# One head load of the last group's own columns, split final sums and shorter bookkeeping in a prefix-sum diagonal kernel

## The chip, the cores and the metric

The kernel runs on one core of one Trainium2 chip. The metric is the device time of one execution in microseconds (us). Of several executions the median is quoted. A profile is one more look at a single execution, whose own time is given beside it. Its engines are TensorE (PE in the lines, PEld for its weight loads), VectorE (DVE), ScalarE (ACT), GpSimd (POOL) and SyncE (SP).

## The reference, cut to what matters

```python
def setup_inputs():
    B, H, W = 4, 4224, 4224
    return {"x": np.random.randn(B, H, W).astype(np.float32)}

def reference(x):
    ps = np.cumsum(np.cumsum(x, axis=1), axis=2)
    diag = np.diagonal(ps, axis1=1, axis2=2)
    return np.cumsum(diag, axis=1).astype(np.float32)
```

Output i of a batch is a sum over the diagonal of the 2-D prefix sum. The kernel never forms the prefix sums. It needs the sum of what each diagonal step adds, which are a column's upper part and a row's left part, and adds those up twice.

## The kernel before

Rows come in strips of 768 (6 blocks of 128), cast to bf16 by the load. Per strip VectorE masks the diagonal block, TensorE sums columns with a one-column selector, and ScalarE and VectorE share the row sums. Eleven groups of 384 columns lie in the rows of one PSUM tile `d`, from which a batch's outputs are made.

The last batch is handled so that little is left after its last byte. Its last 384 rows come last, in small pieces: two blocks of 128 rows (`part_a`), and the last 128 rows as four quarters with each row cut in four (`part_b`). Some of their values come early instead, in a `head` at the very start and in `diag_b`.

```python
    HC = 528
    src_a = x[LB, T0:TB, :].rearrange("(h p) w -> p h w", p=P)
    head = last.tile([P, 2, HC], FP32, name="head")
    nc.sync.dma_start(out=head, in_=src_a[:, :, N - HC : N])
    ...                                   # three strips are prefetched
            if not whole and s == 0:
                diag_b = last.tile([P, P], BF16, name="diag_b")
                nc.gpsimd.dma_start(out=diag_b, in_=x[b, TB:N, TB:N])
```

In the lines, `arows` is the sum of each row of the two blocks, `by` comes from quarter 0 of the last rows, `bsum` from 1 and 2, `esum` from 3, and a *pair sum* (`pair`) is VectorE's sum of a piece, whose halves it adds in one instruction. `dump` is scratch. Row sums of the two blocks are shared. TensorE folds some columns onto 256 by identity matmuls (`fold_a`), ScalarE sums others, VectorE the rest:

```python
            cp, ca = c0 + 768, c0 + 768 + 1152
            fold_in(fold_a, part_a, c0, cp, 256, start=True)      # TensorE
            for h in range(2):
                act_sum(asum[:, h, 1:2], part_a[:, h, cp:ca])     # ScalarE
            row_sums(asum[:, :, 2], part_a[:, :, ca:c1])          # VectorE
```

At the end all row sums are weighed (multiplied by how many times each enters an output) by matmuls into one PSUM tile `fin` and added to the rest. The 32 last outputs have a tile `fin_e` and a store of their own:

```python
        weigh(dtot, weights, M0, start=True)
        weigh(ones_col, by, M0)
        weigh(arows[:, 0:1], weights, 0)
        weigh(arows[:, 1:2], weights, P)
        ...                                   # bsum: sums of quarters 1 and 2
        finish(0, M0)                         # yl[:, :256] = fin + c12
        for k in range(2):
            for i in (1, 0):
                weigh(bsum[:, k, i : i + 1], weights4, M0 + (k + 1) * R)
        ...                                   # esum into fin_e: quarter 3
        finish(M0, GW)                        # yl[:, 256:384]
```

## Time and profile before

| | before |
|---|---|
| time, median of 3 (at the prediction) | 667.96 us (667.37 to 669.88) |
| span of the profiled execution | 665.7 us, timed at 667.42 |
| loads of strips (queue q0) | 99.9% of 16 DMA engines' time |
| busiest engine, VectorE | 334.6 us, 50% |
| last strip packet ends, ye (the last sum) ends | 662.47, 663.68 us |

A queue's share says how much of the 16 DMA engines' time its packets took. The lines themselves are in the prediction. Two quantities make up nearly all of a run's time here: the **stream's end** (when the last strip packet of q0 ends) and the **tail** (from there to the end of `ye`).

Packet times in the prediction, and in the expectations of the first four runs, were counted from a zero that lies 0.31 us off that of the timeline. On the timeline's clock the last packet of before ends at 662.47 us, not 662.77, and the tail is 1.21 us, not 0.9. All other text of this document uses the timeline's clock.

### The profile page before, as it was taken

The page shows a single profiled execution, that of the slowest core. Times are in us where ns is not written, and L with a number is a line of the kernel's source. Part 1 is how long each engine was busy: PE and PEld are TensorE (multiplying, and loading weights), DVE is VectorE, ACT ScalarE, POOL GpSimd, SP SyncE. Part 2 cuts the span into 40 slices and gives each one's busy share as a digit, 9 for nine tenths or more (in the row PEclk, how much of TensorE's full clock was granted, in tenths as well). Part 3 has the DMA queues.
Part 4 walks back from the last instruction along what each step waited for, and adds up shares of the span by engine and source line. Part 5 has one row for each costly group of instructions (what it writes and reads, how often), then busy time and mean ns, then how long its engine had stood idle before and what let it go on. Part 6 is the DMA issues. An engine that isn't in the chain of part 4 may idle for free.

```text
span 665.7 us, 2562 instructions
## 1 busy us (share of the span) xinstructions
PE 204.5 (31%) x981; PEld 97.8 (15%) x981; DVE 334.6 (50%) x165; ACT 140.3 (21%) x226; POOL 31.3 (5%) x59
## 2 busy tenths in 40 slices
PE   0081522403117143130221623504032263250427
PEld 0030211101003021110110311202011031120203
DVE  3161625456916153454782524436288343352767
ACT  0001120406300103040630020304063002030436
POOL 7000000000000000000000000000000000001000
PEclk9995857656558585675755957666565586766758
DMA  9999999999999999999999999999999999999998
GB/s 203 219 219 219 219 218 218 219 212 207 220 221 216 219 219 215 219 215 216 212 219 222 218 215 219 216 216 218 216 213 219 221 213 220 216 216 218 218 207 162
DMA packets 7670, 143.23 MB, mean 215 GB/s; under 512 B 702, under 2 KB 1002, under 8 KB 2154
## 3 DMA queue, kind: packets, MB, share of 16 engines
q0 software_dynamic: 7296, 142.47, 99.9%
q1 hardware_dynamic: 362, 0.61, 0.3%
q8 instruction: 7, 0.11, 0.1%
q14 instruction: 5, 0.04, 0.0%
HBM read 285.47 MB, written 0.07 MB: 429 GB/s over the span
## 4 chain that ended last, share of the span: by engine, by line
DVE 47%; another core or an unknown queue 45%; DMA 5%; PE 2%; issue 1%; DVEq 0%; POOLq 0%
DVE acc L230 29%; DVE mu L320 8%; DVE strip L321 8%; DMA strip<-in_x_dram 5%; PE d L208 1%; DVE c L436 1%; PE fold L208 1%; DVE pu L230 0%; DVE c L250 0%; DVE rows L360 0%; DVE acc L335 0%; PE carry_ps L208 0%; DVE pair L239 0%; PE fin L208 0%
## 5 line engine op out<-in xcount | busy, mean ns | idle before, releaser
L208 PE MATMUL d<-strip,sel 128*11 128x384 bf16 x603 | 138.7, 403 | 377.7 <-DMA strip<-in_x_dram 377.7
L225 ACT ACTIVATE dump<-strip 128x416 bf16<-128x416 bf16 (+8 forms) x112 | 128.4, 1146 | 522.0 <-DMA strip<-in_x_dram 519.3
L320 DVE TENSOR_TENSOR mu<-strip,um 128x4608 bf16<-128x4608 bf16 (+1 forms) x24 | 52.4, 2183 | 307.1 <-DMA strip<-in_x_dram 307.0
L230 DVE TENSOR_REDUCE acc<-strip 128x6 f32<-128x4608 bf16 (+6 forms) x23 | 196.0, 8523 | 0.8
L208 PEld LDWEIGHTS <-sel 128*11 128x11 bf16 x849 | 86.2, 102 | 522.3 <-issue 479.3
L208 PE MATMUL d<-mu,sel 128*11 128x384 bf16 x243 | 49.1, 355 | 45.8 <-DVE mu L320 45.8
L321 DVE TENSOR_TENSOR strip<-strip,mu 128x4608 bf16<-128x4608 bf16 (+1 forms) x24 | 52.4, 2183 | 1.0
L76 POOL DMA_DIRECT2D strip<-in_x_dram x24 | 16.4, 686 | 543.0 <-DVE acc L230 281.7
L225 ACT ACTIVATION_READ_ACCUMULATOR dump<-strip 128x1 f32 x112 | 20.9, 186 | 0.0
L208 PE MATMUL d<-ident,rows 128*11 128x128 f32 x24 | 5.2, 379 | 16.8 <-DVE rows L369 16.8
L208 PE MATMUL fold<-strip,ident_h 128*128 128x480 bf16 x8 | 3.4, 598 | 10.7 <-DMA strip<-in_x_dram 10.7
L208 PE MATMUL d<-halves,rows 128*11 128x64 f32 x48 | 5.5, 296 | 0.0
L94 DVE MEMSET um<- 128x4608 bf16 (+1 forms) x2 | 4.9, 2458 | 1.1 <-issue 1.1
L208 PEld LDWEIGHTS d<-ident,rows 128*11 128x11 f32 x24 | 2.6, 119 | 18.5 <-DVE rows L369 11.7
L95 POOL TENSOR_SCALAR_AFFINE_SELECT um<-um 128x4608 bf16<-128x4608 bf16 (+1 forms) x2 | 5.2, 2611 | 2.4 <-DVE um L94 2.4
L208 PEld LDWEIGHTS d<-halves,rows 128*11 128x11 f32 x48 | 5.1, 134 | 1.5 <-issue 1.5
L230 DVE TENSOR_REDUCE pu<-d 11x1 f32<-11x384 f32 x4 | 2.2, 546 | 5.2 <-PE d L208 5.2
L436 DVE TENSOR_TENSOR_SCAN c<-ones_row,carry,c 11x384 f32<-11x384 f32 x4 | 4.0, 1005 | 0.1
L436 DVE TENSOR_TENSOR_SCAN c<-ones_row,carry,d 11x384 f32<-11x384 f32 x4 | 4.0, 1000 | 0.1
L409 POOL DMA_DIRECT2D strip<-in_x_dram x5 | 2.7, 557 | 26.4 <-DMA strip<-in_x_dram 26.4
L208 PEld LDWEIGHTS <-ident_h 128*128 128x128 bf16 x14 | 1.6, 119 | 13.8 <-issue 13.5
L230 DVE TENSOR_REDUCE parts<-strip 128x3 f32<-128x3072 bf16 x1 | 3.4, 3353 | 0.0
(87 smaller groups left out, 37.2 us busy)
## 6 DMA issues: line engine op xcount, KB each, us to landing
strip<-in_x_dram POOLq DMA_DIRECT2D x19, 6336.0 KB, 76.7
strip<-in_x_dram POOLq DMA_DIRECT2D x5, 3168.0 KB, 59.9
strip<-in_x_dram POOLq DMA_DIRECT2D x1, 1080.0 KB, 49.9
strip<-in_x_dram POOLq DMA_DIRECT2D x1, 768.0 KB, 52.9
strip<-in_x_dram POOLq DMA_DIRECT2D x3, 256.0 KB, 54.1
head<-in_x_dram SPq DMA_DIRECT2D x1, 528.0 KB, 4.0
strip<-in_x_dram POOLq DMA_DIRECT2D x1, 192.0 KB, 43.2
strip<-in_x_dram POOLq DMA_DIRECT2D x1, 64.0 KB, 28.6
```

What stands on the lines that cost most here:

```text
L76: nc.gpsimd.dma_start(out=o, in_=x[b, r0 : r0 + f * P, :].rearrange("(p f) w -> p f w", f=f))
L94: nc.vector.memset(um, 1.0)
L95: nc.gpsimd.affine_select(out=um, in_=um, compare_op=ALU.is_gt, fill=0.0, base=0, pattern=[[-1, f], [1, f * P]], channel_multiplier=-f,)
L208: nc.tensor.matmul(o, lhsT=lhsT, rhs=rhs, start=start, stop=False, skip_group_check=True)
L225: nc.scalar.activation(out=dump[:, :w], in_=src, func=ACT.Copy, accum_out=acc)
L230: nc.vector.reduce_sum(out=acc, in_=src, axis=AX.X)
L320: nc.vector.tensor_mul(out=mu, in0=block, in1=um)
L321: nc.vector.tensor_sub(out=block, in0=block, in1=mu)
L409: nc.gpsimd.dma_start(out=part_b[:, sb, c0:c1], in_=x[b, r0 : r0 + R, :TB].rearrange("r (k c) -> r k c", k=4)[:, :, c0:c1],)
L436: nc.vector.tensor_tensor_scan(out=c12[:, i, :], data0=ones_row, data1=src, initial=carry[:, i : i + 1], op0=ALU.mult, op1=ALU.add,)
```

## The change

The intent is to shorten both ends. The head takes exactly the last group's own 384 columns of all three row blocks, so that `diag_b` with its small packets goes. The final weighed sums lie in two PSUM tiles, so that matmuls into one needn't wait for the addition that reads the other. Sums of halves are written straight to their rows instead of by an addition and a copy. Set-up fills are merged. Shares of the three engines are set anew. The diff, cut to its core:

```diff
-    HC = 528
-    src_a = x[LB, T0:TB, :].rearrange("(h p) w -> p h w", p=P)
-    head = last.tile([P, 2, HC], FP32, name="head")
-    nc.sync.dma_start(out=head, in_=src_a[:, :, N - HC : N])
+    HC = GW
+    NH = N - HC
+    src = x[LB, T0:N, :].rearrange("(h p) w -> p h w", p=P)
+    src_a = src[:, 0:2, :]
+    head = last.tile([P, F, HC], FP32, name="head")
+    nc.sync.dma_start(out=head, in_=src[:, :, NH:N])
 ... (one fill each for the three masks and for ident, ones_col, ones_row)
-            if not whole and s == 0:
-                diag_b = last.tile([P, P], BF16, name="diag_b")
-                nc.gpsimd.dma_start(out=diag_b, in_=x[b, TB:N, TB:N])
 ...
-        sum_up(a6)
-            nc.vector.tensor_copy(
-                out=r6[ps, k : k + 2 * ns : 2, :], in_=a6[ps, :, :, 1]
-            )
+            sum_up(r6[ps, k : k + 2 * ns : 2, :], a6[ps])
 ...
-            wp, ws = 1280, 1280 + 1536
+            wp, ws = 1120, 1120 + 1664
 ...
-            cp, ca = c0 + 768, c0 + 768 + 1152
+            cp, ca = c0 + 256, c0 + 256 + 1600
 ...
-        cp = c0 + 768
+        cp = c0 + 512
 ...
-        fin = psum_s.tile([1, GW], FP32, name="fin")
+        fin_a = psum_s.tile([1, M0], FP32, name="fin_a")
+        fin_b = psum_s.tile([1, P], FP32, name="fin_b")
 ...
-        weigh(dtot, weights, M0, start=True)
-        weigh(ones_col, by, M0)
-        weigh(arows[:, 0:1], weights, 0)
-        weigh(arows[:, 1:2], weights, P)
+        weigh_b(dtot[:, 2:3], weights, M0, start=True)
+        for h in range(2):
+            weigh_a(arows[:, h : h + 1], h * P, start=h == 0)
+        weigh_b(ones_col, by, M0)
+        for h in range(2):
+            weigh_b(arows[:, h : h + 1], weights, h * P)
```

More of the change, by code (lines that the diff above doesn't have):

```diff
@@ L89, with upper_mask @@
     nc.vector.memset(sel[:, NG - 1 : NG], 1.0)
-    def upper_mask(f):
-        um = consts.tile([P, f, f * P], BF16, name=f"um{f}")
-        nc.vector.memset(um, 1.0)
+    um_all = consts.tile([P, (F2 * F2 + F * F + F) * P], BF16, name="um")
+    nc.vector.memset(um_all, 1.0)
+    def upper_mask(f, c0):
+        um = um_all[:, c0 : c0 + f * f * P].rearrange("p (q c) -> p q c", q=f)
         nc.gpsimd.affine_select(
@@ L104, in upper_mask @@
         return um
-    um6 = upper_mask(F2)
-    um3 = upper_mask(F)
-    um1 = consts.tile([P, GW], BF16, name="um1")
-    nc.vector.memset(um1, 1.0)
+    um6 = upper_mask(F2, 0)
+    um3 = upper_mask(F, F2 * F2 * P)
+    um1 = um_all[:, (F2 * F2 + F * F) * P :]
     nc.gpsimd.affine_select(
@@ L118 @@
     )
-    ident = consts.tile([P, P], FP32, name="ident")
-    nc.vector.memset(ident, 1.0)
+    ones_all = consts.tile([P, P + 1 + GW], FP32, name="ones_all")
+    nc.vector.memset(ones_all, 1.0)
+    ident = ones_all[:, :P]
+    ones_col = ones_all[:, P : P + 1]
+    ones_row = ones_all[:NG, P + 1 :]
     nc.gpsimd.affine_select(
@@ L133 @@
     halves = consts.tile([P, HP], FP32, name="halves")
-    nc.vector.tensor_add(out=halves, in0=ident[:, :HP], in1=ident[:, HP:])
-    ones_row = consts.tile([NG, GW], FP32, name="ones_row")
-    nc.vector.memset(ones_row, 1.0)
+    nc.gpsimd.tensor_add(out=halves, in0=ident[:, :HP], in1=ident[:, HP:])
     def counted(name, rows, width, pieces):
@@ L213 @@
     nc.vector.tensor_copy(out=weights4_h, in_=weights4)
-    ones_col = consts.tile([P, 1], FP32, name="ones_col")
-    nc.vector.memset(ones_col, 1.0)
     def fold_in(o, src, c0, c1, w, start=False):
@@ L274 @@
     asum = last.tile([P, 2, 5], FP32, name="asum")
-    dtot = last.tile([P, 1], FP32, name="dtot")
+    dtot = last.tile([P, F], FP32, name="dtot")
     hs = last.tile([P, 3], FP32, name="hs")
@@ L278 @@
     hmu = last.tile([P, 3, GW], BF16, name="hmu")
-    row_sums(hs[:, 0:2], head)
-    for h in range(2):
+    row_sums(hs, head)
+    for h in range(F):
         w = GW - h * P
-        masked(hmu[:, h, :w], head[:, h, HC - w : HC], um1[:, :w], hu[:, h : h + 1])
-    nc.vector.tensor_sub(out=asum[:, :, 0], in0=hs[:, 0:2], in1=hu[:, 0:2])
+        masked(hmu[:, h, :w], head[:, h, HC - w :], um1[:, :w], hu[:, h : h + 1])
+    nc.vector.tensor_sub(out=dtot, in0=hs, in1=hu)
+    nc.gpsimd.tensor_copy(out=asum[:, :, 0], in_=dtot[:, 0:2])
     for b in range(B):
@@ L331, with sum_up @@
         nc.vector.memset(acc6[:, 0, :, 0], 0.0)
-        def sum_up(acc):
-            nc.vector.tensor_add(
-                out=acc[..., 1], in0=acc[..., 1], in1=acc[..., 0]
-            )
+        def sum_up(o, acc):
+            nc.vector.tensor_add(out=o, in0=acc[..., 0], in1=acc[..., 1])
         ns = NS if whole else NS - 1
@@ L345 @@
             add_up(strip, F2, s * F2 * P, acc6[:, s], um6)
-            if not whole and s == 0:
-                diag_b = last.tile([P, P], BF16, name="diag_b")
-                nc.gpsimd.dma_start(out=diag_b, in_=x[b, TB:N, TB:N])
             if not whole and s == 1:
-                row_sums(hs[:, 2:3], diag_b)
-                masked(hmu[:, 2, :P], diag_b, um1[:, :P], hu[:, 2:3])
-                nc.vector.tensor_sub(out=dtot, in0=hs[:, 2:3], in1=hu[:, 2:3])
-                for h in range(3):
+                for h in range(F):
                     columns(LG, h * P, GW, hmu[:, h, : GW - h * P])
         a6 = acc6[:, :ns]
-        sum_up(a6)
         for h in range(2):
@@ L359 @@
             k = row_of(h)
-            nc.vector.tensor_copy(
-                out=r6[ps, k : k + 2 * ns : 2, :], in_=a6[ps, :, :, 1]
-            )
+            sum_up(r6[ps, k : k + 2 * ns : 2, :], a6[ps])
         strip = strip_tile()
@@ L367 @@
             add_up(strip[:, :F], F, T0, acc3[:, 0], um3)
-            sum_up(acc3[:, 0])
-            nc.vector.tensor_copy(out=r3[:, LG, :], in_=acc3[:, 0, :, 1])
+            sum_up(r3[:, LG, :], acc3[:, 0])
         else:
@@ L375 @@
             add_up(strip[:, :F], F, T0 - 2 * GW, acc3[:, 0], um3)
-            sum_up(acc3[:, 0])
-            nc.vector.tensor_copy(out=r3[:, row_of(LG - 2), :], in_=acc3[:, 0, :, 1])
+            sum_up(r3[:, row_of(LG - 2), :], acc3[:, 0])
             fold_g = psum_s.tile([P, F, 160], FP32, name="fold")
-            wp, ws = 1280, 1280 + 1536
+            wp, ws = 1120, 1120 + 1664
             fold_in(fold_g, strip[:, F:], 0, wp, 160, start=True)
@@ L394 @@
             part_a = strip[:, 0:2]
-            part_b = strip[:, 2, :TB].rearrange("p (s c) -> p s c", s=4)
-            acuts = [(1536, N - HC), (0, 1536)]
+            part_b = strip[:, 2, :NH].rearrange("p (s c) -> p s c", s=4)
+            acuts = [(1536, NH), (0, 1536)]
             for c0, c1 in acuts:
                 nc.gpsimd.dma_start(out=part_a[:, :, c0:c1], in_=src_a[:, :, c0:c1])
-            CB = TB // 4
-            bcut = 768
+            CB = NH // 4
+            bcut = CB - 256
             for sb, c0, c1 in (
@@ L410 @@
                     out=part_b[:, sb, c0:c1],
-                    in_=x[b, r0 : r0 + R, :TB].rearrange("r (k c) -> r k c", k=4)[
+                    in_=x[b, r0 : r0 + R, :NH].rearrange("r (k c) -> r k c", k=4)[
                         :, :, c0:c1
@@ L464, with weigh_a, weigh_b, finish @@
         E0 = GW - R
-        fin = psum_s.tile([1, GW], FP32, name="fin")
+        fin_a = psum_s.tile([1, M0], FP32, name="fin_a")
+        fin_b = psum_s.tile([1, P], FP32, name="fin_b")
         fin_e = psum_s.tile([1, R], FP32, name="fin_e")
         yl = last.tile([1, GW], FP32, name="yl")
-        def weigh(rows, w, r0, start=False):
-            matmul(fin[:, r0:], rows, w[:, : GW - r0], start=start)
-        def finish(c0, c1):
+        def weigh_a(rows, r0, start=False):
+            matmul(fin_a[:, r0:], rows, weights[:, : M0 - r0], start=start)
+        def weigh_b(rows, w, r0, start=False):
+            lo = max(r0, M0)
+            matmul(fin_b[:, lo - M0 :], rows, w[:, lo - r0 : GW - r0], start=start)
+        def finish(src, c0, c1):
             nc.vector.tensor_add(
-                out=yl[:, c0:c1], in0=fin[:, c0:c1], in1=c12[0:1, 1, c0:c1]
+                out=yl[:, c0:c1], in0=src, in1=c12[0:1, 1, c0:c1]
             )
@@ L481 @@
         for c in range(0, CB, P):
-            matmul(by_ps, part_b[:, 0, c : c + P], weights4_h, start=c == 0)
+            w = min(P, CB - c)
+            matmul(by_ps[:w], part_b[:, 0, c : c + w], weights4_h, start=c == 0)
         by = last.tile([P, P], FP32, name="by")
         nc.scalar.copy(out=by, in_=by_ps)
-        weigh(dtot, weights, M0, start=True)
-        weigh(ones_col, by, M0)
-        weigh(arows[:, 0:1], weights, 0)
-        weigh(arows[:, 1:2], weights, P)
+        weigh_b(dtot[:, 2:3], weights, M0, start=True)
[4 more added lines that the diff above has]
+            weigh_b(arows[:, h : h + 1], weights, h * P)
         bsum = last.tile([P, 2, 2], FP32, name="bsum")
-        for k, ca in ((0, 512), (1, 448)):
+        for k, ca in ((0, 480), (1, 416)):
             act_sum(bsum[:, k, 0:1], part_b[:, k + 1, :ca])
             pair_sum(bsum[:, k, 1:2], part_b[:, k + 1, ca:])
-        finish(0, M0)
+        finish(fin_a, 0, M0)
         for k in range(2):
             for i in (1, 0):
-                weigh(bsum[:, k, i : i + 1], weights4, M0 + (k + 1) * R)
+                weigh_b(bsum[:, k, i : i + 1], weights4, M0 + (k + 1) * R)
         esum = last.tile([P, 3], FP32, name="esum")
-        act_sum(esum[:, 0:1], part_b[:, 3, :320])
-        pair_sum(esum[:, 1:2], part_b[:, 3, 320:bcut])
+        act_sum(esum[:, 0:1], part_b[:, 3, :288])
+        pair_sum(esum[:, 1:2], part_b[:, 3, 288:bcut])
         pair_sum(esum[:, 2:3], part_b[:, 3, bcut:])
@@ L506 @@
             matmul(fin_e, esum[:, k : k + 1], weights4[:, :R], start=k == 1)
-        finish(M0, GW)
+        finish(fin_b, M0, GW)
         nc.sync.dma_start(
```

## The prediction

> **What bounds the kernel now.** I read the page's totals first, then its row of slices and the DMA queues.
>
> ```profile
> PE 204.5 (31%) x981; PEld 97.8 (15%) x981; DVE 334.6 (50%) x165; ACT 140.3 (21%) x226; POOL 31.3 (5%) x59
> DMA  9999999999999999999999999999999999999998
> q0 software_dynamic: 7296, 142.47, 99.9%
> q1 hardware_dynamic: 362, 0.61, 0.3%
> HBM read 285.47 MB, written 0.07 MB: 429 GB/s over the span
> ```
>
> No engine is busy for more than half of the span, the DMA row is 9 in all slices but the last, and queue q0 (the loads of strips, cast to bf16 on the way) alone fills 99.9% of the 16 DMA engines. 285.47 MB is 4 x 4224 x 4224 x 4 bytes: each input value is read once and none can be saved. So the time is: start until the stream of strips begins, the stream, and what follows the last byte. Work of VectorE, ScalarE or TensorE inside the stream costs nothing as long as strips are freed in time, and VectorE idles 307 us before its first multiplies of strips, waiting for loads. Only the two ends and the length of the stream are open to this change.
>
> The start, from the DMA view of the first 8 us, by queue: packets, MB, share of 16 engines' time.
>
> ```profile
> q0 software_dynamic: 46, 1.17, 69.1%
> q1 hardware_dynamic: 272, 0.54, 22.7%
> ```
>
> q1 is the head: 256 packets of 2112 bytes and 16 tiny ones that signal the end. In the trace's packet records the head runs from 2.20 to 4.75 us (median 86 ns a packet), and the first strip packet starts on each engine between 4.05 and 4.75 us. From there q0 has no hole up to 662.77 us.
>
> The tail, from the timeline of the last microseconds: start, length, instruction, idle time before it.
>
> ```profile
> 659.52 0.19 ACT L225 ACTIVATION_READ_ACCUMULATOR dump<-strip 128x1 f32 x1
> 660.15 0.16 DVE L230 TENSOR_REDUCE arows<-asum 128x2 f32<-128x10 f32 x1
> 661.58 0.58 ACT L225 ACTIVATE dump<-strip 128x448 bf16<-128x448 bf16 x1 [0.56 <-DMA strip<-in_x_dram]
> 661.90 0.41 DVE L474 TENSOR_TENSOR yl<-fin,c 1x256 f32<-1x256 f32 x1
> 662.37 0.71 PE L208 MATMUL fin<-weights,bsum 128*1 128x96 f32 x8 [0.76 <-DVE yl L474]
> 662.46 0.39 DVE L239 SCALAR_TENSOR_TENSOR pair<-strip 128x224 f32<-128x224 bf16 x1 [0.15 <-DMA strip<-in_x_dram]
> 662.78 0.29 DVE L239 SCALAR_TENSOR_TENSOR pair<-strip 128x128 f32<-128x128 bf16 x1
> 662.92 0.50 PE L208 MATMUL fin_e<-weights,esum 128*1 128x32 f32 x6
> 663.12 0.28 DVE L474 TENSOR_TENSOR yl<-fin,c 1x128 f32<-1x128 f32 x1
> 663.50 0.18 DVE L512 TENSOR_TENSOR ye<-fin_e,yl 1x32 f32<-1x32 f32 x1
> 663.71 0.24 SPq L513 DMA_DIRECT2D out_dram<-ye  x1
> ```
>
> From the last packet (662.77) to the last sum (663.68) there is 0.9 us, then about 2 us for the output to land. The span is 665.7 us and its run was timed at 667.42; the other timed runs lie up to 669.88. That 1.7 us and the scatter are not touched by the change.
>
> **What the Trainium skill says.**
> 1. "DMA: Bandwidth & Descriptors", section "Why small descriptors are slow (HBM only)": every packet has a fixed overhead beside its bytes. The trace agrees and sizes it: q0 packets of 256, 512, 1536, 2048, 3072, 4320 and 25344 bytes take 41, 60, 135, 173, 248, 340 and 1886 ns, which is 22 ns + 0.0736 ns a byte for all of them.
> 2. The same page, "Queues, rings and completion order": an engine takes turns between the queues that have work for it, packet by packet. The trace agrees in that head and strips overlap from 4.05 to 4.75 us; so more head work is shared out, not free, once strips are there.
> 3. "PSUM — Partial Sum Buffer", "PSUM bank collisions raise a hardware error": accesses are to be guarded by bank and quadrant. The trace shows such an order at the tile fin: the matmuls of bsum waited 0.76 us for the addition that read fin, though it read other columns.
>
> **The change part by part.**
>
> Stream, per engine (16 engines, so 128 packets are 8 on each). The loads in q0 lose the columns that the head now takes. Removed: diag_b, 8 packets x 41 ns and one signal of 22 ns, 0.35 us. The first piece of the 256 rows grows from 4320 to 4608 bytes, 16 x 21 ns = +0.34 us. The quarter-row pieces shrink from 2048 to 1920 bytes (24 x 9.4 = -0.23 us) and from 1536 to 1408 (8 x 9.4 = -0.08 us). The pieces of 3072 and 512 bytes stay. Sum: -0.32 us.
>
> Head: 384 packets of 1536 bytes for 256 of 2112. Taking 63 ns (in proportion to bytes) to 78 ns (what q1's output packets of 1536 bytes took), an engine spends 24 x 0.070 = 1.68 us for 16 x 0.086 = 1.38 us: +0.30 us. If it all delays the strips, the stream ends where it did. If the strips' own start sets 4.05 us and the head fits before it, up to 0.3 us is gained. The engines are at most half used from 2.2 to 3.2 us (51 head packets start there, against 185 in the next microsecond), so a little may be absorbed. I take the stream's end as 0.1 us earlier, between -0.3 and +0.2.
>
> Set-up: memsets are merged, halves goes to GpSimd. The large mask's fill is 6144 instead of 4608 columns, 3.90 x 6144/4608 = 5.2 us, so the masks come about 1.3 us later. They are first needed at 34.8 us: no cost.
>
> The sums straight to their rows: in each batch three or more small VectorE instructions of 0.16 to 0.18 us go, in all 15 rows fewer in the instruction order. They lie in time in which VectorE waits for loads: no gain in the end. Moving diag_b's sums to the start takes 0.8 us from VectorE at 571.5 us, which also waits for loads after that.
>
> Tail: ScalarE gets more columns. From its 0.84 us at 768 and 1.48 at 1536, an activation costs 0.20 us + 0.83 ns a column, and the next starts 0.13 us after its end. The two sums of 1600 columns are 1.54 us each instead of 1.16, the two of 1024 columns 1.06 instead of 0.84. Counting from the piece of 3072 bytes, which ends some 0.1 us later than before in the stream, these end at about 660.4 instead of 659.7, so arows comes at 660.45 instead of 660.15. Then ScalarE copies by until 660.65, sums bsum's first part until 661.25 and meets the second at its data, near 661.55. So it has caught up 1 us before the end. TensorE then has 2 x (256 + 128) columns for fin_a, 2 x 128 for by and 4 x 128 for fin_b, at 0.85 ns a column (weight loads of the 384-column ones are 0.32 us apart) some 1.4 us with the latency, so until 662.05. The matmuls of bsum no longer wait for the addition at 661.90, so the first half is done before the second half's sum is there, at 662.2 to 662.4. fin_b is complete near 662.75 instead of 663.08. But the addition into yl can't start before VectorE has done its last pair sum (663.07), which hangs on the last packet. So of 0.33 us on TensorE only the gap of 0.04 us and the queueing in front of fin_e count: VectorE's chain gets 0.02 us from 208 columns for 224, and ye starts about 0.05 to 0.1 us earlier after the last byte.
>
> Sum: stream -0.1, tail -0.07, together about **-0.2 us** of 668.
>
> **The rivals.**
> - *The PSUM split is worth its whole wait.* 0.76 us of TensorE's idle time is named after the addition, and the chain of waits runs through fin and yl. Against it: at 663.12 VectorE had been free only since 663.07. It would make 667.2.
> - *The wider head hurts.* The first head packets took up to 842 ns and every one left behind when strips begin has to alternate with packets of 1886 ns. If descriptors, not bytes, set the head's pace, 384 of them take half as long again: 1.3 us later at worst, 669. For it: the head's 2.5 us is more than its 1.4 us of packets. Against it: sharing delays the head, which no one needs before VectorE's set-up at 17 us, and leaves the sum of work in the engines alone.
> - *ScalarE becomes the bound of the tail.* If an activation is slower than the line through its lengths, by and bsum slip and pass esum's data at 662.4. A slip of 0.3 us gives 668.2. Against: the 0.56 us of idle time before bsum's second part is a reserve that I have used only 0.35 us of.
>
> **Range and chances.** All mechanisms lie within +-1.3 us, and the timed runs of before span 2.5 us. Prediction 667.7 us, from 667.96 less 0.2 and rounded; range 666.7 to 669.2, which is wider upwards since the runs scatter upwards and the head may hurt. 2% would be 13 us, and nothing here reaches it: same 0.98, faster 0.01, slower 0.01.
>
> **What would show it.** Right: q0 again at 99.9%; 384 head packets near 70 ns that end 0.2 to 0.5 us later, with the first strip packets 0 to 0.3 us later; no 256-byte packets in q0; the last strip packet within 0.3 us of 662.77; arows near 660.45; no wait of the bsum matmuls for yl; the last addition still right behind the last pair sum. Wrong: a hole in q0, strips that start over 0.5 us later, a second bsum activation that doesn't wait for its data, or a span that differs by over 1.3 us.

## The result, and the profile after

The changed kernel took 669.25 us (median of 6, 668.02 to 670.94). Before took 668.66 us in 6 runs that include the 3 known earlier (667.28 to 670.29). The ratio is 1.001 with a 95% interval of 0.9987 to 1.0033. Ratios here are worked out from the fast runs of both kernels in the same rounds, and are not quite the ratio of the medians. All outputs are right. The median lies 0.05 us above the predicted range.

The totals, the DMA row and the queues of the changed kernel, from its page:

```profile
PE 206.6 (31%) x981; PEld 99.1 (15%) x981; DVE 333.0 (50%) x150; ACT 141.5 (21%) x226; POOL 31.3 (5%) x60
DMA  9999999999999999999999999999999999999997
q0 software_dynamic: 7152, 142.44, 99.6%
q1 hardware_dynamic: 490, 0.66, 0.3%
HBM read 285.47 MB, written 0.07 MB: 428 GB/s over the span
```

VectorE has 15 instructions fewer, as the diff says, and q0 has 144 packets fewer: the 128 of `diag_b` and its 16 signals. The bytes read are the same, and the kernel is bound by the stream as before. The start, from the DMA view of the first 8 us:

```profile
q0 software_dynamic: 43, 1.09, 65.1%
q1 hardware_dynamic: 400, 0.59, 25.1%
```

There are 384 head packets and 16 signals, and q0 has got a little less far by 8 us. The end has changed more. These are stretches of 1 us of before: its start and end, its length, busy time (and instructions) of PE, PEld, DVE, ACT and POOL, TensorE's granted clock, DMA share, GB/s.

```profile
660.00:661.00 1.00, 0.98 (x4) 0.22 (x5) 0.56 (x4) 0.71 (x2) 0.00 (x0) 1.00 1.12 202
661.00:662.00 1.00, 0.61 (x3) 0.08 (x1) 0.48 (x3) 0.44 (x2) 0.00 (x0) 1.00 0.91 158
662.00:663.00 1.00, 0.64 (x10) 0.61 (x10) 0.85 (x5) 0.73 (x4) 0.00 (x0) 1.00 0.17 23
663.00:664.00 1.00, 0.41 (x8) 0.14 (x5) 0.54 (x4) 0.08 (x1) 0.00 (x0) 1.00 0.00 0
```

And the same of the changed kernel:

```profile
661.00:662.00 1.00, 0.52 (x3) 0.09 (x2) 0.47 (x3) 1.00 (x4) 0.00 (x0) 0.71 1.02 173
662.00:663.00 1.00, 1.00 (x5) 0.40 (x4) 0.40 (x4) 0.52 (x3) 0.00 (x0) 0.50 0.39 58
663.00:664.00 1.00, 1.00 (x6) 0.63 (x5) 0.83 (x6) 0.80 (x4) 0.00 (x0) 0.50 0.05 7
664.00:665.00 1.00, 1.00 (x10) 0.77 (x8) 0.15 (x2) 0.06 (x1) 0.00 (x0) 0.59 0.00 0
```

In before the clock is 1.00 and TensorE has idle time. In the changed kernel the clock falls to 0.50 between 661 and 662 us, TensorE is then busy without a gap, and it still works when VectorE and ScalarE are nearly done. Some lines of its timeline there:

```profile
661.53 0.16 DVE L232 TENSOR_REDUCE arows<-asum 128x2 f32<-128x10 f32 x1 [0.59 <-ACT dump L227]
661.75 1.44 PE L212 MATMUL fin_a<-weights,arows 128*1 128x256 f32 x4 [0.48 <-DVE arows L232]
662.99 0.63 PE L212 MATMUL fin_b<-by,ones_all 128*1 128x128 f32 x2
663.41 1.06 PE L212 MATMUL fin_b<-weights,arows 128*1 128x128 f32 x4
663.86 0.28 DVE L241 SCALAR_TENSOR_TENSOR pair<-strip 128x128 f32<-128x128 bf16 x1
664.27 0.99 PE L212 MATMUL fin_b<-weights,bsum 128*1 128x96 f32 x8
665.29 0.28 DVE L469 TENSOR_TENSOR yl<-fin_b,c 1x128 f32<-1x128 f32 x1 [1.15 <-PE fin_b L212]
665.68 0.18 DVE L510 TENSOR_TENSOR ye<-fin_e,yl 1x32 f32<-1x32 f32 x1
```

The last addition into yl waited 1.15 us for TensorE, after a last pair sum that was ready at 664.15. In before it started right behind that sum. So between these two executions the time goes as follows: timed 669.64 against 667.42, +2.22 us, of which the stream's end is 663.48 against 662.47 (+1.01) and the tail 2.38 against 1.21 (+1.17). Which of both belongs to the change, and which to one execution's luck, is what the experiments are about.

### The profile page after: what moved, and what is told of

It is laid out like the page before. It is cut to its first block, busy times and chain, and to the rows that moved or that the text cites. A ratio compares the mean times of both kernels' runs of the same rounds, so it can differ in the third digit from the quotient of the medians.

```text
span 667.9 us, 2547 instructions
## 1 busy us (share of the span) xinstructions
PE 206.6 (31%) x981; PEld 99.1 (15%) x981; DVE 333.0 (50%) x150; ACT 141.5 (21%) x226; POOL 31.3 (5%) x60
## 3 DMA queue, kind: packets, MB, share of 16 engines
q0 software_dynamic: 7152, 142.44, 99.6%
## 4 chain that ended last, share of the span: by engine, by line
another core or an unknown queue 77%; ACT 21%; issue 1%; PE 1%; DVE 0%; ACTq 0%; DVEq 0%
ACT dump L227 21%; PE fin_b L212 0%; PE fin_a L212 0%; ACT L227 0%; ACTq L227 0%; DVE yl L469 0%; DVE ye L510 0%; DVE arows L232 0%; DVEq L232 0%; DVEq L510 0%
## 5 line engine op out<-in xcount | busy, mean ns | idle before, releaser
L227 ACT ACTIVATE dump<-strip 128x416 bf16<-128x416 bf16 (+7 forms) x112 | 129.8, 1159 | 521.7 <-DMA strip<-in_x_dram 519.0
L212 PE MATMUL d<-mu,sel 128*11 128x384 bf16 x243 | 50.7, 363 | 43.4 <-DVE mu L323 43.4
L212 PE MATMUL d<-ones_all,rows 128*11 128x128 f32 x24 | 5.2, 380 | 16.4 <-DVE rows L338 16.1
L94 DVE MEMSET um<- 128x6144 bf16 x1 | 5.2, 5178 | 1.2 <-issue 1.2
L212 PEld LDWEIGHTS d<-ones_all,rows 128*11 128x11 f32 x24 | 2.5, 119 | 18.4 <-DVE rows L338 16.9
L426 DVE TENSOR_TENSOR_SCAN c<-ones_all,carry,c 11x384 f32<-11x384 f32 x4 | 4.0, 1006 | 0.1
L426 DVE TENSOR_TENSOR_SCAN c<-ones_all,carry,d 11x384 f32<-11x384 f32 x4 | 4.0, 1000 | 0.1
L232 DVE TENSOR_REDUCE parts<-strip 128x3 f32<-128x3168 bf16 x1 | 3.5, 3453 | 0.0
```

The lines of the kernel that those rows point to most:

```text
L94: nc.vector.memset(um_all, 1.0)
L212: nc.tensor.matmul(o, lhsT=lhsT, rhs=rhs, start=start, stop=False, skip_group_check=True)
L227: nc.scalar.activation(out=dump[:, :w], in_=src, func=ACT.Copy, accum_out=acc)
L232: nc.vector.reduce_sum(out=acc, in_=src, axis=AX.X)
L426: nc.vector.tensor_tensor_scan(out=c12[:, i, :], data0=ones_row, data1=src, initial=carry[:, i : i + 1], op0=ALU.mult, op1=ALU.add,)
```

## The experiments

The theory: (1) the wider head delays the stream about as much as the saved packets shorten it; (2) the tail grows because TensorE's clock is halved just before its final matmuls. The Trainium skill ("TensorE: Matmul & The Clock Gate", "Part 1: The HAM clock gate (the "warmup" mystery)") describes two clock states, half and full, switched by how busy TensorE was in a free-running window of 3413 ns. The traces agree with the states and the window: all clock records are 0.50 or 1.00, and within a trace the changes lie whole multiples of 3.41 us apart (in the changed kernel 654.58, 661.41, 664.82 us). By the new shares TensorE folds 256 + 512 columns of `part_a` in place of 768 + 768, just ahead of that. The rivals: the order and the split make the chain long, later row sums from ScalarE are all of it, or it is scatter of single executions.

Fourteen profiles came of it. The twelve runs were made in three sets, each on another chip with runs of the kernel before beside them: `after_again`, `before_again`, `old_cuts` and `warm`; then `before_warm`, `before_cuts`, `warm_one_fin` and `two_blocks`; then the other four. Low clock is the time at 0.50 among the last ones before `ye`; "none" means 1.00 to the end of `ye` from a rise between 653.9 and 656.9 us.

| run | stream's end | low clock | tail | timed |
|---|---|---|---|---|
| before | 662.47 | none | 1.21 | 667.42 |
| before_again | 663.00 | 660.23 to 663.64 | 2.08 | 668.80 |
| before_third | 662.34 | none | 1.24 | 667.27 |
| changed | 663.48 | 661.41 to 664.82 | 2.38 | 669.64 |
| after_again | 662.69 | 658.92 to 665.75 | 2.73 | 669.22 |
| after_third | 663.50 | 658.87 to 662.28 | 1.13 | 668.43 |
| old_cuts | 663.78 | none | 1.10 | 668.69 |
| warm | 663.13 | none | 1.14 | 667.95 |
| filled_old_cuts | 662.62 | none | 1.09 | 667.53 |
| before_warm | 664.16 | none | 1.17 | 669.01 |
| before_cuts | 664.55 | 659.88 to 663.29 | 1.57 | 669.83 |
| before_cuts_2 | 662.86 | 659.62 to 663.03 | 2.25 | 668.81 |
| warm_one_fin | 663.96 | none | 1.46 | 669.40 |
| two_blocks | 664.76 | none | 1.14 | 669.94 |

### after_again and before_again: the two kernels once more, unchanged

No edit.

> The changed kernel once more, unchanged, for a second profile and ten times as a measure of scatter. Theory (the tail): between the last strip packet and the end of the last sum (ye) lie 2.07 us, against 0.91 us before, because TensorE's granted clock falls to 0.50 near 661.7 us, just as its chain of final matmuls begins, and ScalarE brings arows later. The clock should fall again and the tail be 1.9 to 2.2 us. Rival (scatter): the fall was luck of that execution; then this profile may show the clock at 1.00 to the end and a tail under 1.4 us. Time: ratio to before 0.999 to 1.004 by both.

Measured: 668.84 us (6 runs), ratio 1.0006 (0.999 to 1.0021). The clock fell again, at 658.92, and the tail was 2.73 us. (The 1.9 to 2.2 expected are 2.2 to 2.5 on the right clock, so the tail was longer than expected.) So the fall was not that one execution's.

> The kernel before once more, unchanged. Theory: TensorE's granted clock is 1.00 up to the end of the sums and the tail from last strip packet to the end of ye is 0.85 to 1.0 us. Rival (scatter): the clock falls in this one, and its tail grows to 1.3 us or more. The ratio of the same kernel against itself shows what this method can tell apart: 0.998 to 1.002.

Measured: 668.11 us (4 runs), ratio 0.9996 (0.9976 to 1.0017). This one missed: the clock fell in the kernel before too, and the tail was 2.08 us. The timeline of VectorE shows it:

```profile
662.48 0.08 DVE L239 DVE_READ_ACCUMULATOR pair<-strip 128x1 f32 x1
663.31 0.41 DVE L474 TENSOR_TENSOR yl<-fin,c 1x256 f32<-1x256 f32 x1 [0.75 <-PE fin L208]
```

The first addition, which was not kept waiting in the first profile of before, waits 0.75 us for the matmuls of arows, which took 2.34 us at half clock against 1.24 at full. So a fallen clock is no property of the changed kernel alone, and here it cost the kernel before about 0.9 us. It follows that one profile of each could not have told the two kernels apart.

### old_cuts: the old shares in the changed kernel

```diff
-            wp, ws = 1120, 1120 + 1664
+            wp, ws = 1280, 1280 + 1536
-            cp, ca = c0 + 256, c0 + 256 + 1600
+            cp, ca = c0 + 768, c0 + 768 + 1152
-        cp = c0 + 512
+        cp = c0 + 768
```

> The changed kernel with the shares of TensorE and ScalarE in the last group's sums as they were before (folds of 1280, 768 and 768 columns, sums of 1536 and 1152). Theory (tail by clock and by late arows): TensorE has its fold matmuls back in the window before 661.7 us, so the clock stays 1.00, arows come about 0.4 us sooner, and the tail is 0.9 us, some 1.1 us less than in the changed kernel; the ratio to before goes to 0.997 to 1.000. Rival (the order and the split into fin_a and fin_b make the chain long, whatever came before): the tail stays near 2 us.

Measured: 668.17 us (6 runs), ratio 0.9992 (0.9977 to 1.0007). Clock 1.00, tail 1.10 us (1.2 was expected on the right clock). Order and split are the changed kernel's, so that rival falls.

### warm: TensorE's idle time filled, nothing else

Six matmuls with zero weights add 0 to `fold_a`. They have no use but to keep TensorE busy.

```diff
+    zero_h = consts.tile([P, P], BF16, name="zero_h")
+    nc.vector.memset(zero_h, 0.0)
         matmul(carry_ps[:, 1:2], apart, pu[:, 0:1])
+        if not whole:
+            for _ in range(4):
+                matmul(fold_a, zero_h, um_all[:, :512].rearrange("p (h c) -> p h c", h=2))
         fold_in(fold_a, part_a, c0, cp, 256)
+        for _ in range(2):
+            matmul(fold_a, zero_h, um_all[:, :512].rearrange("p (h c) -> p h c", h=2))
```

> The changed kernel with six more matmuls by zero weights on TensorE (four after the carry, two after the last fold), which add 0 to fold_a and fill idle time of TensorE between 658 and 660.2 us; cuts, order and data flow are the changed kernel's. Theory (clock): the granted clock stays 1.00 until the end and the tail falls to 1.2 to 1.5 us (arows still late). Rival (arows late is all of it): the tail stays at 1.9 us or more, even at full clock. A third possibility: the clock falls all the same, and then this run tells nothing of the rest.

Measured: 668.18 us (6 runs), ratio 0.9994 (0.9979 to 1.0009). Clock 1.00, tail 1.14 us, which is less than the 1.5 to 1.8 expected on the right clock. The timeline:

```profile
661.20 0.16 DVE L234 TENSOR_REDUCE arows<-asum 128x2 f32<-128x10 f32 x1 [0.63 <-ACT dump L229]
661.42 0.81 PE L214 MATMUL fin_a<-weights,arows 128*1 128x256 f32 x4 [0.47 <-DVE arows L234]
662.72 0.72 PE L214 MATMUL fin_b<-weights,bsum 128*1 128x96 f32 x8
663.46 0.29 DVE L243 SCALAR_TENSOR_TENSOR pair<-strip 128x128 f32<-128x128 bf16 x1
663.68 0.27 DVE L476 TENSOR_TENSOR yl<-fin_b,c 1x128 f32<-1x128 f32 x1
```

The arows are as late as in the changed kernel (1.93 us ahead of the stream's end at 663.13, against 1.95). But fin_a's matmuls take 0.81 us in place of 1.44, and the last addition starts right behind the last pair sum. So late arows alone cost next to nothing with the split (1.14 against 1.10 in old_cuts); the clock costs it.

### before_warm: the same filling in the kernel before

The edit is that of `warm`, with the first 512 columns of `um6`.

> The kernel before with the same six matmuls by zero weights that filled TensorE's idle time in the run called warm. (Times here are on the timeline's clock; those of the packets in the prediction and in the expectations of the first four runs were 0.31 us late, so their tails of 0.91 and 2.07 us are 1.2 and 2.4 us.) Theory: the clock fell in one of two profiles of the kernel before too, and the tail then was 2.1 us in place of 1.2; what counts is how busy TensorE is in each 3.41 us window, and where the windows lie is chance. With the idle time filled the clock stays 1.00 until the end and the tail is 1.1 to 1.25 us; the median falls to 667.3 to 668.0 and the ratio to 0.998 to 1.000. Rival (the fall belongs to the new kernel's order): no difference to before, ratio 1.000 and the same scatter.

Measured: 667.89 us (6 runs), ratio 0.9991 (0.9973 to 1.0008). Clock 1.00, tail 1.17 us, as the theory says. The median is inside what it expects, but the interval doesn't tell it from the rival's 1.000.

### before_cuts and before_cuts_2: only the new shares, in the kernel before

The edit is that of `old_cuts` the other way round, in the kernel before.

> The kernel before with nothing but the new shares of TensorE and ScalarE in the last group's sums (folds of 1120, 256 and 512 columns in place of 1280, 768 and 768). Theory: these cuts take about 1 us from TensorE between 655 and 660 us, so that a window of 3.41 us there is busy for 0.55 or less; the clock falls before the final matmuls in this execution as in both of the changed kernel, the tail is 1.9 to 2.8 us, and the ratio is 1.0005 to 1.0025. Rival (the fall comes from the split or from the wider head): clock and tail as in the kernel before, chance of a fall about one half.

Measured: 668.74 us (6 runs), ratio 1.0003 (0.9982 to 1.0024). The clock fell, but a window early: it was at full again from 663.29, ahead of the last packet at 664.55. The tail was 1.57 us, less than expected. Little of it need be the clock's: with one tile and the new shares the tail is 1.46 us even at full clock (`warm_one_fin`, below).

> The kernel before with nothing but the new shares, for the second time. In the first the clock fell at 659.88 us and was back at 663.29, ahead of the last packet (664.55), and the tail was 1.57 us. Theory: the clock falls again; the tail is 1.5 to 2.8 us, by how long the low clock lasts into the final matmuls. Rival: no fall, tail as in the kernel before, 1.2 us.

Measured: 668.77 us (4 runs), ratio 0.9997 (0.9975 to 1.0019). The clock fell again, and the tail was 2.25 us. In the windows:

```profile
656.00:658.00 2.00, 0.65 (x6) 0.36 (x6) 1.41 (x5) 1.74 (x4) 0.00 (x0) 1.00 1.09 209
658.00:660.00 2.00, 1.18 (x10) 0.69 (x9) 1.96 (x3) 1.80 (x3) 0.00 (x0) 0.90 1.11 207
660.00:662.00 2.00, 2.00 (x9) 0.58 (x8) 1.03 (x5) 1.44 (x6) 0.00 (x0) 0.50 1.06 189
```

TensorE is busy for 0.65 of 2 us at first, and half a clock is what it has left by 660. With the shares alone, without the split or the head, the clock fell in 2 of 2. The times don't resolve it; the profiles do, as far as their small number goes (below).

### warm_one_fin: filled, but with one tile for the final sums

In `warm`, fin_a and fin_b are one tile again, in the old order.

```diff
-        weigh_b(dtot[:, 2:3], weights, M0, start=True)
-        for h in range(2):
-            weigh_a(arows[:, h : h + 1], h * P, start=h == 0)
-        weigh_b(ones_col, by, M0)
-        for h in range(2):
-            weigh_b(arows[:, h : h + 1], weights, h * P)
+        weigh(dtot[:, 2:3], weights, M0, start=True)
+        weigh(ones_col, by, M0)
+        for h in range(2):
+            weigh(arows[:, h : h + 1], weights, h * P)
```

> The run called warm with one PSUM tile in place of fin_a and fin_b, and with the order of the kernel before (dtot, by, rows); the rest, with the six matmuls by zero weights, is the same. At full clock warm had a tail of 1.14 us. Theory (prediction's step on the split): the split frees TensorE early but the last addition waits for VectorE's last pair sum anyway, so the tail here is 1.15 to 1.3 us, though the bsum matmuls wait for the addition that reads the tile. Rival (the split is worth its wait): the tail is 1.6 us or more. Should the clock fall, the tail is 2 us and more and the run says less.

Measured: 669.02 us (4 runs), ratio 1.0005 (0.9986 to 1.0024). At full clock the tail was 1.46 us, between the two forecasts.

```profile
663.64 0.41 DVE L471 TENSOR_TENSOR yl<-fin,c 1x256 f32<-1x256 f32 x1
664.11 0.71 PE L214 MATMUL fin<-weights,bsum 128*1 128x96 f32 x8 [0.50 <-DVE yl L471]
664.86 0.28 DVE L471 TENSOR_TENSOR yl<-fin,c 1x128 f32<-1x128 f32 x1 [0.27 <-PE fin L214]
```

The matmuls of bsum wait 0.50 us for the addition, and the last addition waits 0.27 us for them. With the new shares the split, with its order, is thus worth 0.32 us (1.46 less 1.14, one profile each). With the old shares it has little to win: 1.17 to 1.24 us with one tile (before_warm, before, before_third), 1.09 and 1.10 with two.

### two_blocks: a narrower head

In `warm`, the head has two row blocks (256 packets of 1536 bytes), and the third block's columns come through q0 in the last batch.

```diff
-    head = last.tile([P, F, HC], FP32, name="head")
-    nc.sync.dma_start(out=head, in_=src[:, :, NH:N])
+    head = last.tile([P, 2, HC], FP32, name="head")
+    nc.sync.dma_start(out=head, in_=src_a[:, :, NH:N])
+    head_c = last.tile([P, GW], BF16, name="head_c")
+            if not whole and s == 0:
+                nc.gpsimd.dma_start(out=head_c, in_=x[LB, TB:N, NH:N])
```

> The run called warm with two row blocks in the head in place of three: 256 packets of 1536 bytes at the start; the third block's 384 columns are loaded by the strips' queue in the middle of the last batch, as diag_b was. Theory (the wider head delays the strips): the first 16 strip packets start on average at 3.93 to 3.96 us in the kernel before and at 4.17 to 4.24 in the kernels with the wide head; here they start at 3.7 to 3.95, and q0 carries 128 packets of 768 bytes more, 0.63 us an engine, so that the stream's end is 0.2 to 0.5 us later than in warm. Rival (the strips' own descriptors set their start): they start at 4.1 to 4.25 as in warm.

Measured: 669.99 us (4 runs), ratio 1.0016 (0.9996 to 1.0037). The first 16 strip packets start on average at 3.85 us, within the theory's range and ahead of warm's 4.24. The stream ends 1.63 us later than in warm, of which the theory explains at most 0.5; the rest is scatter, below. The effect of the head's width on the start is of the size of the scatter as well. Six profiles with the old head have 3.93, 3.96, 3.96, 3.96, 4.05 and 4.32 us (mean 4.03), seven with the wide one 4.16 to 4.38 (mean 4.23). So the wide head's +0.20 us is likely and not certain.

### after_third, before_third and filled_old_cuts: counting, and the candidate

No edit in the first two.

> The changed kernel for the third time. Theory: its shares leave a 3.41 us window of TensorE at 0.55 busy or less for most positions of the windows, so the clock falls again before the last addition and the tail is 1.9 to 2.8 us (1.5 if the clock recovers in time). Rival (chance alone, one half each): a clock of 1.00 and a tail of 1.14 us.

Measured: 668.3 us (4 runs), ratio 1.0000 (0.9981 to 1.0018). The clock fell for the third time in three, but it recovered in time:

```profile
658.00:660.00 2.00, 1.02 (x6) 0.21 (x3) 1.78 (x3) 1.62 (x3) 0.00 (x0) 0.72 1.11 205
660.00:662.00 2.00, 1.86 (x12) 0.97 (x12) 1.41 (x5) 1.97 (x6) 0.00 (x0) 0.50 1.01 174
662.00:664.00 2.00, 2.00 (x20) 1.41 (x18) 1.33 (x8) 1.42 (x6) 0.00 (x0) 0.93 0.15 23
```

The final matmuls from 662.28 on ran at 1.00 and the tail was 1.13 us, so the expected tail missed (1.5 was named for this case). It is the same kernel with the same late arows as in the profiles with 2.38 and 2.73, and what differs is when the clock was low. That is the plainest evidence for the clock.

> The kernel before for the third time; so far the clock fell in one profile of two. Theory: it falls if a window lies over the gaps from about 656.8 to 660.2 us, which is chance: tail 1.2 us at full clock, 2.1 us else. Either outcome counts only for how often it happens; a tail near 1.2 us with a fallen clock, or near 2 us at full clock, would speak against the clock as the cause.

Measured: 667.35 us (4 runs), ratio 0.9985 (0.9967 to 1.0003) of a kernel against itself. Full clock, tail 1.24 us.

> The candidate for the best of all: the changed kernel with the old shares of TensorE and ScalarE (as in old_cuts) and the six matmuls by zero weights (as in warm). Theory: clock at 1.00 to the end and a tail of 1.05 to 1.2 us, as each of the two alone gave (1.10 and 1.14); the time is then set by the scatter of the stream's end, so the ratio to before is 0.998 to 1.000 and not to be told from 1. Rival (the two get into each other's way: later carry, later arows): tail of 1.4 us or more.

Measured: 668.5 us (6 runs), ratio 0.9995 (0.998 to 1.001). Full clock, tail 1.09 us, the shortest of all. It is not told from before by its time.

### What decides the fall, and what is left open

From the clock records and the times of matmuls of all 14 traces I took every full-clock window of 3.41 us (some 720) with the share in which a matmul was running. No window with 0.56 or more ended in a fall, and every window with 0.41 or less did. In between, some 40 windows held, all but one in the body of the kernel (two_blocks has one of 0.54 that spans the end of `ye`), and six did not, five of which are windows of the tail with 0.46 to 0.55. There TensorE runs many short matmuls whose ends are modelled, so the profile's busy share is not quite what the chip counts. From half clock it rises after windows of 0.78 or more, with two exceptions (0.81 and 0.83). The new shares leave 0.37 to 0.55 in the window that matters in 5 of 5 profiles without filling; the old shares without filling did so in 1 of 4 (before_again, 0.53); the filled kernels, in none of 5. Where the windows lie differs from run to run, so these are frequencies from small counts. A 3.41 us window laid anywhere from the rise of the clock to the end of `ye` would be busy for at least 0.84 in filled_old_cuts, but in warm_one_fin for as little as 0.53: the filling alone does not rule a fall out, the filling with the old shares seems to.

Open: what makes the stream's end scatter from 662.34 to 664.76 us. In the traces the large packets take 1886 ns, and the surplus of those that take longer adds up to between 0.18 us (before_third) and 1.05 us (two_blocks) for each engine. It does not go with the change: its mean is 0.46 us in the six profiles with the old head and 0.49 in the seven with the wide one. What slows those packets was not tried.

## Why the prediction was right or wrong

**What bounds the kernel: right.** q0 took 99.6%, the bytes are the same, and no engine's work inside the stream showed in the time. The 15 VectorE instructions saved bring nothing that could be seen.

**Stream: the sums right, the end not told from scatter.** q0's packets other than the large ones sum to 15.84 us an engine after and 16.14 before: -0.30 for the -0.32 of the prediction, in all profiles of both kernels. The head's packets took 65 ns (median) where 70 was taken, and the sum of the head went from 1.80-1.92 to 1.95-2.00 us an engine, +0.1 for +0.30 predicted. The head ended 0.1 us later (0.2 to 0.5 was named), and the strips began 0.24 us later (0 to 0.3 was named; both means of the three profiles of each kernel). One reading behind this was wrong: from 2.2 to 3.2 us on the prediction's clock 70 head packets start, not 51, and packets fill 0.75 of the 16 engines' time, so the engines were not "at most half used" and had little room to absorb a larger head. The stream's mean end over the 16 engines was about 0.1 us later when the surplus of slowed packets is taken off, inside -0.3 to +0.2; this is an estimate, since the trace does not name a packet's engine and the packets had to be strung together by their times. The end itself came later in the changed kernel, by 0.62 us on the mean of the three profiles of each (663.48, 662.69 and 663.50 against 662.47, 663.00 and 662.34), where 0.3 was named as the limit. That this is scatter is likely and not shown: the seven profiles with the wide head have a mean of 663.31 us, the six with the old one 663.23.

**Arows: right.** They were predicted 0.3 us later and came 1.95, 1.92 and 1.95 us ahead of the stream's end, in before 2.32, 2.45 and 2.35: 0.4 later. ScalarE did catch up: bsum's second sum waited 0.48 us for its data.

**The step that failed is the tail**: "TensorE then has ... columns ... at 0.85 ns a column", "so until 662.05", and "fin_b is complete near 662.75 ... only the gap of 0.04 us ... count". The rate was read in a trace where the clock was 1.00, and the working took it as fixed, though it took work from TensorE just ahead of it. The chain from fin_a to the last matmul of arows, predicted at 1.4 us, took 1.46 us at full clock (warm, 661.42 to 662.88) and 2.72 at half (the changed kernel, 661.75 to 664.47). At half clock fin_b was complete at 665.26, 1.78 us after the stream's end, and the tail was 2.38 and 2.73 us in two profiles of three. The size predicted for full clock, -0.07 us, is near what the profiles show whose final matmuls ran at full clock (1.13 and 1.14 for 1.21 and 1.24). So the arithmetic was right and its assumption wrong. Of the four conditions named as showing it wrong one came true (the spans differ by 2.2 us), but none named the clock. None of the three rivals named it either. The rival "ScalarE becomes the bound" had the right place, the shares, for a wrong reason.

**The rival of the split** was set aside for the right reason with the old shares (about 0.1 us there) and not with the new: with those it wins 0.32 us, which pays for arows that come later.

**Range: wrong at its base.** 667.96 was a median of three (less 0.2 it is 667.76, which was written as 667.7). Over runs of before it is 668.32 (39 runs, 667.21 to 670.77), and 668.66 in the six quoted with the result. The expected change of -0.2 was measured as +0.1% (0.7 us), +0.06% and 0.00% in three sets of rounds, each with an interval that holds 0. "Same" was right. In one set of rounds the changed kernel took 668.96 us on average and old_cuts and warm 668.01 and 668.14 (6 runs each), which is about the size that a lost clock costs; the intervals of their ratios to before still overlap, and in the third set the changed kernel and filled_old_cuts differ by only 0.35 us (668.59 and 668.24). So the clock is shown as the cause of the longer tail, not of the whole time's place above the range.

## What to carry to other kernels

Before taking work from TensorE to balance a tail, look at its granted clock in that stretch: work that seems to fill idle time may be what keeps the clock up for the short matmuls that end the kernel. Where a rate is read from one trace, ask under which clock it was measured and whether the change leaves that clock alone. For changes under 0.5% read the parts that can be timed inside a trace (stream's end, tail), in several profiles of each kernel, since total times of one kernel scattered here by over 3 us.

## What the Trainium skill lacked or had wrong

- "TensorE: Matmul & The Clock Gate", "Part 1: The HAM clock gate (the "warmup" mystery)", gives as the condition of a fall, in its table of states, "after ≥1 idle window". Here the clock fell after windows that were far from idle: shares of 0.37 to 0.55 in the tails of 6 profiles, and never at 0.56 or more. The same part does tell of a kernel whose short idle times between groups of matmuls made the clock oscillate, but it gives no share for either direction; the rise here took 0.78 or more.
- The same page's practical rule ("Why this matters for your kernels"), to leave no idle gaps over about 3 us, was not enough: the longest gap of TensorE from 655 to 661 us in the changed kernel was 0.98 us between matmuls, and the clock was lost.
- No page gives a packet's duration for loads that cast float32 to bf16 in this queue: 22 ns + 0.0736 ns a byte written, from 256 to 25344 bytes.
